# A two-layer decoder trunk: gates projected with the values, values in three column passes, background work at other turns

## The chip, the core and the metric

The kernel runs on one core of a Trainium2 chip. PE is the matmul engine, DVE the vector engine, ACT the scalar engine, POOL is GpSimd, and SP issues most DMAs. The metric is the device time of one execution in microseconds (us). Before the change three runs gave a median of 2369.42 us (2369.24 to 2374.68).

## What is computed

A trunk of two layers over 1024 tokens of 1024 features, in fp32. Layer 0 is an mLSTM, a matrix memory worked on in chunks of 128 tokens, followed by a squared-ReLU MLP. Layer 1 is causal attention over a shared low-rank K/V, followed by an MLP. Scales and shifts of the norms come from a conditioning vector. The part that the change touches most:

```
q, k, v, ig, fg, og = split(h @ w_in)        # 512, 512, 1024, 8, 8, 1024 columns
i_pre = ig + gate_b[0];  f_pre = fg + gate_b[1]
# per chunk of 128 tokens and per head (8 heads, dk 64, dv 128):
log_d   = b[t] - b[s] + i[s], -inf where s > t   # b: running sum of log sigmoid(f)
w_intra = exp(log_d - m[t])
s       = (q k^T) * w_intra
num     = w_inter * (q C) + s v
C_new   = decay * C + sum_s w[s] k[s] v[s]^T     # the state carried to the next chunk
h       = num / max(|den|, exp(-m))
out     = (rmsnorm(h) * sigmoid(og)) @ w_out
```

In layer 1 a block of 128 queries scores against the keys up to its own last token, so the last piece of keys is 128, 256, 384 or 512 wide.

## The kernel before

Tokens are worked on in two halves of 512 (`hfs[0]`, `hfs[1]`, called half 0 and half 1). Every large product is in three matmuls on a high and a low part of each operand (`mm3`, L230 to L234: L232, L233, L234). A weight tile is loaded by `wload` into a `raw` buffer (four of them), ACT casts its high part (L189), DVE subtracts to get the low part (L190), and the pair goes to a `ws` buffer (eight, so four pairs). In most projections the weight is the stationary operand and 512 tokens stream; in V the tokens are stationary and 256 weight columns stream.

PSUM has three pools of two tiles: `ps` and `pc` (one bank each) and `pm` (two banks each). Instructions are recorded step by step by generators, and a scheduler then places them into one queue for each engine, which runs in order. `weave` and `in_turn` take turns between two generators; `with_bg(g, bgs, n)` takes n steps of the background generator for each step of g. The background holds the scales and shifts of the norms (`ada_chunk`, DVE multiply-adds L358 and L360 over weight rows, then four transposes L340).

The stages of layer 0, by time in the trace of before:

- q and k of half 0 (to 80 us), then its gates: `gates_in` (L626) puts 16 gate columns in a weight tile of 128 mostly zero columns and runs 16 matmuls of L642 and L643 for a half, each 512 wide; `gates0` (L702) then computes on 8 partitions.
- V of half 0 (`v_in`, L657) from 84 to 147 us, taken in turns with `intra0` (L761). For each head `intra0` puts a row of gate sums (L775) and the causal mask (L772, bf16) into one PSUM bank, ACT takes exps (L779); for each pair of heads it makes 64-row scores (L787), which DVE multiplies by the exps (L792).
- `og0` (L690), the output gate, taken in turns with `chunks0` (L814), to 217 us. In `chunks0` the 64-row products with the state are L831, the 128-row products L836.
- gates, q and k, then V of half 1, with `split_o` (L801) of half 0 between.
- the first MLP, half 0, from about 540 to 846 us. `two_streams` (L2028) steps the dense generator `f0` and another one in turns. There the other is `behind` (L2078), which draws steps from `bg_latent`: the rest of the background, then `latent_weights` (L1322), which has six turns. A turn loads a weight tile, sums its rows on DVE (L1336, L1338 seven times), scales it (L1341), splits it (L190), then turns the sums with a transpose (L1346) and reduces them (L1347). In the trace they run between 736 and 804 us. `with tc.issue_after` in `go` (L2011) keeps PE's order as recorded.

In layer 1, `score_mm` (L1506) makes five matmuls for each piece of keys (L1517 to L1520, L1523), and a piece is at least 256 wide.

Of the kernel before, what the change touches and what calls it, by code (L numbers as in the profile page):

```python
# [9 lines left out]
F32 = mybir.dt.float32  # L10
# [72 lines left out]
def kernel(  # L83
# [542 lines left out]
    def gates_in(hf):  # L626
        h = hf.h
        wg = raw(F32R).rearrange("p (a b) -> p a b", b=P)
        nc.gpsimd.memset(wg.bitcast(F32), 0.0)
        rg = tmp()  # L630
        rgv = rg[:, :128].rearrange("p (k n) -> p k n", n=16)
        nc.sync.dma_start(rgv, wcols(w_in, 2048, 16))
        for g in range(2):
            s = ts(g, 8)
            nc.scalar.copy(wg[:, :, 32 * g : 32 * g + 8], rgv[:, :, s])
            nc.vector.tensor_sub(
                wg[:, :, 64 + 32 * g : 72 + 32 * g], rgv[:, :, s],
                wg[:, :, 32 * g : 32 * g + 8].bitcast(F32),
            )
        gp = ps()  # L640
        for k in range(KD):
            nc.tensor.matmul(gp, wg[:, k], h.lo[k], start=k == 0, stop=False)  # L642
# [14 lines left out]
    def v_in(hf):  # L657
        h = hf.h
        hf.v = []
        last = sb.tile([P, 4, VE], F32, tag="v8", bufs=1, name=f"v8_{next(uid)}")  # L660
        nc.gpsimd.memset(last[:, :, 128:VE], 1.0)
        for t in range(4):
            v = k4()[:, : 7 * VE].rearrange("p (h e) -> p h e", e=VE)
            nc.gpsimd.memset(v[:, :, 128:VE], 1.0)
            hf.v.append([v[:, h_] for h_ in range(7)] + [last[:, t]])
            hf.v[t].append(v)
        for j in range(4):
            w0 = wload([(0, 0, wcols(w_in, 1024 + j * 256, 256, 0, 4))], 256)
            w1 = wload([(0, 0, wcols(w_in, 1024 + j * 256, 256, 4, 4))], 256)
            for t in range(4):  # L670
                pt = ps()[:, :256]
                for k in range(KD):
                    w = w0 if k < 4 else w1
                    mm3(
                        pt, h.hi[k][:, ts(t, P)], h.lo[k][:, ts(t, P)],
                        w[0][:, k % 4], w[1][:, k % 4], k == 0, k == KD - 1,
                    )
                i = pt.rearrange("p (a b) -> p a b", b=P)
                if j < 3:
                    parts = [(hf.v[t][8][:, 2 * j : 2 * j + 2, 0:128], i)]  # L680
                else:
                    parts = [(hf.v[t][6 + e][:, 0:128], i[:, e]) for e in range(2)]
                for o, a in parts:
                    if t % 2:
                        nc.vector.tensor_copy(o, a)
                    else:
                        nc.scalar.copy(o, a)
                yield

    def og0(hf, alloc):  # L690
        hf.gs = FH(F32, alloc)
        for k in range(NH):
            pt = proj_fm(w_in, 2064 + k * P, hf.h)
            g = hf.gs[k]
            nc.scalar.activation(g, pt, AF.Exp, scale=-1.0)  # L695
# [6 lines left out]
    def gates0(hf):  # L702
# [3 lines left out]
        t1, t2, t3 = r8(), r8(), r8()  # L706
        nc.vector.tensor_copy(t1, gp[64:72])
        nc.vector.scalar_tensor_tensor(t1, gp[0:8], col(GB, 1)[0:8], t1, ALU.add, ALU.add)
        nc.vector.tensor_copy(t2, gp[96:104])
        nc.vector.tensor_copy(t3, gp[32:40])  # L710
        nc.vector.scalar_tensor_tensor(t2, t3, col(GB + 1, 1)[0:8], t2, ALU.add, ALU.add)
        ig, fg = t1, t2
# [48 lines left out]
    def intra0(hf):  # L761
# [3 lines left out]
        for p_ in range(4):  # L765
# [3 lines left out]
            for r in range(2):  # L769
                hh = 2 * p_ + r  # L770
                pt = pc()
                nc.tensor.matmul(  # L772
                    pt, maskA, identb.unsqueeze(1).to_broadcast([P, 4, P]), start=True, stop=False
                )
                nc.tensor.matmul(  # L775
                    pt, e8[:, hh : hh + 1].to_broadcast([P, P]), RM, start=False, stop=True
                )
# [5 lines left out]
                yield  # L783
            st = pm()
            for j in range(4):
                for r in range(2):
                    nc.tensor.matmul(  # L787
                        st[:, r, ts(j, P)], kp[ts(r, 64), ts(j, P)], qp[ts(r, 64), ts(j, P)],
                        start=True, stop=True,
                    )  # L790
            for r in range(2):
                nc.vector.tensor_mul(PT[:, r], st[:, r], E[r])  # L792
                yield
            pt = pc()
            nc.tensor.matmul(pt, selW[:, p_], RM, start=True, stop=True)
# [18 lines left out]
    def chunks0(hf):  # L814
# [4 lines left out]
        for j in range(4):  # L819
            g = hf.i * 4 + j  # L820
            cs = ts(j, P)
            v = hf.v[j]
            nvs = []
            for q in range(2):
                num = pm()
                nv = num[:, :, 0 : 2 * VE].rearrange("p b (i e) -> p b i e", e=VE)
                for i in range(2):
                    p_ = 2 * q + i

                    for r in range(2 if g > 0 else 0):  # L830
                        nc.tensor.matmul(  # L831
                            nv[:, r, i], hf.q[p_ // 2][ts(r, 64), p_ % 2, cs],
                            Cst[ts(r, 64), p_], start=True, stop=False,
                        )
                    for r in range(2):
                        nc.tensor.matmul(  # L836
                            nv[:, r, i], hf.PT[p_][:, r, cs], v[2 * p_ + r],
                            start=g == 0, stop=True,
                        )
                nvs.append(nv)  # L840
            if g < 7:
# [664 lines left out]
    def score_mm(o2, kk, q, kn, i):  # L1506
# [424 lines left out]
    drain(with_bg(gates_in(hfs[0]), bgs, 1))  # L1931
    x1 = load_x1()
    drain(weave(with_bg(v_in(hfs[0]), bgs, 1), intra0(hfs[0]), 1.5))
    y1 = rms_x1(x1)
# [36 lines left out]
    so = split_o(hfs[1])  # L1971
    for k, _ in enumerate(og0(hfs[1], k4v)):
        if k % 2:
# [53 lines left out]

    def two_streams(dense, other, fill=iter(()), more=4):  # L2028

# [4 lines left out]
        while True:  # L2034
# [5 lines left out]
            while n == "align" and at[0] != "hid" or n != "align" and n > 0:  # L2040
# [60 lines left out]
    drain(p1)  # L2101
    two_streams(with_weight_sums(f0), behind(bg_latent(), 4))
    rope_perm()
# [132 lines left out]
```

## Time and profile before

| | |
|---|---|
| median of three runs | 2369.42 us |
| the profiled execution | 2373.3 us |
| its span | 2371.2 us |
| mean granted PE clock | 0.996 |
| DMA, mean | 177 GB/s |

The page lists the busy time of each engine over the span, the chain of work that ended last, and the costliest groups of instructions. A row of a group reads: line, engine, operation, output <- inputs, shape, count | busy us, mean ns of one | idle time before them and what ended it. PE matmuls overlap, so the mean of one is longer than the step from one start to the next. A row of the timeline reads: start, length, engine, line, operation, and in brackets the idle time before it. A row of the waits reads: total us, times, longest.

### The profile page before, as it was taken

Reading aid. Unit: us, or ns where it says so; the run is one execution under the profiler, and the core shown is the slowest. Engines: PE = TensorE matmul, PEld = TensorE weight load, DVE = VectorE, ACT = ScalarE, POOL = GpSimd, SP = SyncE. Lnnn points to the kernel's source line nnn. Section 1 sums busy time; section 2 is a strip of 40 time slices with the busy share of each in tenths; the row PEclk is TensorE's granted clock in tenths of the full one; section 3 lists DMA queues with packets and bytes.
Section 4 is the critical chain, followed back from the end, with each engine's and each line's share of the span. In section 5 each row is a group of like instructions: output and inputs, shape, how many; then the busy total and the mean of one; then the engine's idle time right before and its main releaser. Section 6 shows DMA issues by size and latency. Waiting matters only on the chain.

```text
span 2371.2 us, 32533 instructions
## 1 busy us (share of the span) xinstructions
PE 2334.8 (98%) x12197; PEld 1967.3 (83%) x12197; DVE 1605.2 (68%) x2657; ACT 1099.8 (46%) x1826; POOL 147.6 (6%) x345
## 2 busy tenths in 40 slices
PE   7999999999999999999999999999999999999998
PEld 5888888788888888888888888888888888989997
DVE  6667866868666677877774967766566478457556
ACT  4355334655333464434444544434434445655543
POOL 1000000000001210111110110001001000000000
PEclk9999999999999999999999999999999999999999
DMA  9453564544656966667754675885544552657552
GB/s 312 143 145 89 181 184 137 170 130 150 187 178 166 313 184 197 185 200 205 227 157 117 196 208 176 269 272 167 173 129 132 147 169 86 189 175 218 165 183 89
DMA packets 408350, 420.77 MB, mean 177 GB/s; under 512 B 27427, under 2 KB 310112, under 8 KB 404608
## 3 DMA queue, kind: packets, MB, share of 16 engines
q1 hardware_dynamic: 402272, 385.02, 51.9%
q0 software_dynamic: 5920, 33.66, 6.5%
q8 instruction: 96, 1.57, 0.3%
q14 instruction: 62, 0.51, 0.1%
HBM read 359.37 MB, written 92.80 MB: 191 GB/s over the span
## 4 chain that ended last, share of the span: by engine, by line
PE 90%; DVE 4%; DMA 3%; ACT 2%; issue 1%; SPq 0%; DVEq 0%; ACTq 0%
PE ps L232 16%; PE ps L233 15%; PE ps L234 15%; PE pm L232 10%; PE pm L233 10%; PE pm L234 10%; PE pc L234 2%; PE pc L232 2%; PE pc L233 2%; DMA raw<-in_mlp_w_dram 1%; PE pc L1637 1%; DMA raw<-in_a_w_in_dram 1%; DVE wl L190 1%; PE pm L836 1%; PE pm L1523 1%
## 5 line engine op out<-in xcount | busy, mean ns | idle before, releaser
L190 DVE TENSOR_TENSOR wl<-raw,wh 128x1024 fp32r<-128x1024 f32 (+2 forms) x382 | 458.5, 1203 | 385.8 <-ACT wh L189 281.4
L189 ACT CAST wh<-raw 128x1024 fp32r<-128x1024 f32 (+2 forms) x382 | 394.0, 1035 | 657.9 <-PE ps L232 241.8
L232 PE MATMUL ps<-k,wl 128*128 128x512 f32 (+1 forms) x1464 | 560.3, 383 | 2.6 <-ACT k L695 1.4
L234 PE MATMUL ps<-k,wh 128*128 128x512 f32 (+1 forms) x1464 | 551.6, 377 | 0.0
L233 PE MATMUL ps<-k,wh 128*128 128x512 f32 (+1 forms) x1464 | 550.7, 376 | 0.0
L232 PEld LDWEIGHTS ps<-k,wl 128*128 128x128 f32 x1464 | 275.7, 188 | 56.5 <-issue 3.6
L234 PEld LDWEIGHTS ps<-k,wh 128*128 128x128 f32 x1464 | 275.5, 188 | 51.7 <-issue 0.7
L233 PEld LDWEIGHTS ps<-k,wh 128*128 128x128 f32 x1464 | 275.9, 188 | 50.0 <-issue 1.9
L198 DVE TENSOR_TENSOR k<-k,pm 128x512 f32<-128x512 f32 (+1 forms) x254 | 211.2, 860 | 87.2 <-PE pm L234 86.1
L232 PE MATMUL pm<-hd,wl 128*128 128x512 f32 x512 | 201.1, 393 | 0.5 <-ACT hd L472 0.5
L233 PE MATMUL pm<-hd,wh 128*128 128x512 f32 x512 | 199.5, 390 | 0.2 <-DVE hd L473 0.2
L234 PE MATMUL pm<-hd,wh 128*128 128x512 f32 x512 | 199.4, 390 | 0.0
L232 PE MATMUL pm<-wh,hd 128*128 128x512 f32 x488 | 192.2, 394 | 3.9 <-ACT raw L1529 3.7
L233 PE MATMUL pm<-wl,hd 128*128 128x512 f32 x488 | 190.5, 390 | 0.0
L234 PE MATMUL pm<-wh,hd 128*128 128x512 f32 x488 | 190.3, 390 | 0.0
L360 DVE SCALAR_TENSOR_TENSOR tma<-raw,cond,tma 128x512 f32<-128x512 f32 x168 | 125.7, 748 | 20.0 <-DMA raw<-in_kv_ada_w_dram 13.8
L1529 ACT ACTIVATE raw<-pm,sm 128x128 f32<-128x128 f32 (+3 forms) x64 | 47.4, 741 | 155.1 <-DVE sm L1528 118.2
L473 DVE TENSOR_TENSOR hd<-tmp,hd 128x512 fp32r<-128x512 f32 x128 | 88.0, 689 | 40.4 <-ACT hd L472 39.8
L232 PEld LDWEIGHTS pm<-hd,wl 128*128 128x128 f32 x512 | 96.2, 188 | 20.9 <-ACT hd L472 0.9
L233 PEld LDWEIGHTS pm<-hd,wh 128*128 128x128 f32 x512 | 96.2, 188 | 20.5 <-DVE hd L473 0.5
L234 PEld LDWEIGHTS pm<-hd,wh 128*128 128x128 f32 x512 | 96.2, 188 | 20.2
L985 POOL COPY sm<-sm 128x1 f32<-128x1 f32 x128 | 51.9, 412 | 967.2 <-DVE sm L984 930.3
(385 smaller groups left out, 4064.1 us busy)
## 6 DMA issues: line engine op xcount, KB each, us to landing
raw<-in_mlp_w_dram SPq DMA_DIRECT2D x240, 512.0 KB, 4.3
raw<-in_ada_w_dram SPq DMA_DIRECT2D x80, 512.0 KB, 4.3
raw<-in_a_w_in_dram SPq DMA_DIRECT2D x48, 512.0 KB, 4.8
sums<-in_mlp_w_dram POOLq DMA_DIRECT2D x96, 256.0 KB, 4.8
raw<-sums SPq DMA_DIRECT2D x64, 256.0 KB, 3.7
xs<-k SPq DMA_DIRECT2D x40, 256.0 KB, 3.6
raw<-in_kv_ada_w_dram SPq DMA_DIRECT2D x16, 512.0 KB, 3.9
raw<-in_a_w_out_dram SPq DMA_DIRECT2D x16, 512.0 KB, 5.0
```

The source lines that it names most:

```text
L189: nc.scalar.copy(hi[:, :n], r[:, :n])
L190: i = nc.vector.tensor_sub(lo[:, :n], r[:, :n], hi[:, :n].bitcast(F32))
L198: return f(*a, **k)
L232: nc.tensor.matmul(o, ll, rh, start=start, stop=False, **m)
L233: nc.tensor.matmul(o, lh, rl, start=False, stop=False, **m)
L234: pe_last[0] = nc.tensor.matmul(o, lh, rh, start=False, stop=stop, **m)
L360: nc.vector.scalar_tensor_tensor(acc, r[:, kk], cond[:, k : k + 1], acc, ALU.mult, ALU.add)
L473: nc.vector.tensor_sub(lo, u, hi.bitcast(F32))
L836: nc.tensor.matmul(nv[:, r, i], hf.PT[p_][:, r, cs], v[2 * p_ + r], start=g == 0, stop=True,)
L985: now = nc.gpsimd.tensor_copy(seen, flag)
L1523: nc.tensor.matmul(o[:, :w], qh, kh, start=False, stop=True)
L1529: nc.scalar.activation(pr[:, :n], f, AF.Exp, bias=m, scale=SCALE, accum_out=l)
```

## The change

The gates' 16 columns are taken along as columns 256 to 271 of V's first pass, with tokens stationary, and turned by four transposes for each half. V is made in three passes, of 2, 3 and 3 heads, into two `pm` tiles. The mask matmul goes; POOL sets the values after the diagonal to zero, behind the product with the scores. The scores of a pair go to two `ps` banks. `chunks0` issues its 64-row products by fours, then its 128-row products by fours. Every second `og0` tile of half 1 goes to a `pm` bank. `score_mm` takes 128 columns where there are no more. The background has other rates, in half 1 it runs from q and k on, `behind` aligns once at its start, and takes two steps of the background a turn where it took four.

```diff
     def gates_in(hf):
...
-        gp = ps()
-        for k in range(KD):
-            nc.tensor.matmul(gp, wg[:, k], h.lo[k], start=k == 0, stop=False)
-            nc.tensor.matmul(gp, wg[:, k], h.hi[k], start=False, stop=k == KD - 1)
+        gp = pc()
+        for t in range(4):
+            nc.tensor.transpose(gp[0:64, ts(t, P)], hf.graw[:, t], ident)
         hf.gp = gp
...
+        for h0, nh, kg in ((6, 2, 3), (0, 3, 2), (3, 3, 2)):
+            n = nh * P + (16 if h0 == 6 else 0)
+            b = [pm(), pm()]
+            for k0 in range(0, KD, kg):
+                nk = min(kg, KD - k0)
+                w = wload([(0, 0, wcols(w_in, 1024 + h0 * P, n, k0, nk))], n)
+                for t in range(4):
+                    for k in range(nk):
+                        kk = k0 + k
+                        mm3(
+                            b[t // 2][:, t % 2, :n], h.hi[kk][:, ts(t, P)], h.lo[kk][:, ts(t, P)],
+                            w[0][:, k], w[1][:, k], kk == 0, kk == KD - 1,
+                        )
...
-    def og0(hf, alloc):
+    def og0(hf, alloc, wide=False):
...
-            pt = proj_fm(w_in, 2064 + k * P, hf.h)
+            pt = proj_fm(w_in, 2064 + k * P, hf.h, (lambda: pm()[:, 0]) if wide and k % 2 else ps)
...
                 nc.tensor.matmul(
-                    pt, maskA, identb.unsqueeze(1).to_broadcast([P, 4, P]), start=True, stop=False
-                )
-                nc.tensor.matmul(
-                    pt, e8[:, hh : hh + 1].to_broadcast([P, P]), RM, start=False, stop=True
+                    pt, e8[:, hh : hh + 1].to_broadcast([P, P]), RM, start=True, stop=True
                 )
...
-            st = pm()
+            st = [ps(), ps()]
...
+            causal = PT.rearrange("p r (j t) -> p (r j) t", t=P)
+            nc.gpsimd.affine_select(
+                out=causal, in_=causal, pattern=[[0, 8], [1, P]], compare_op=ALU.is_ge,
+                fill=0.0, base=0, channel_multiplier=-1,
+            )
...
-            w = max(256, min(512, n - g * 512))
+            w = min(512, n - g * 512)
...
-    drain(gates_in(hfs[1]))
-    main = chain(twice(qk_in(hfs[1])), v_in(hfs[1]))
-    for _ in range(4):
+    v1 = v_in(hfs[1])
+    for _ in range(6):
+        next(v1)
+    main = chain(with_bg(twice(qk_in(hfs[1])), bgs, 1.6), with_bg(v1, bgs, 1.1))
+    scored = chain(gates_in(hfs[1]), intra0(hfs[1]))
+    next(scored)
+    for n in range(8):
         next(main)
-    drain(split_o(hfs[0]))
-    for _ in range(2):
-        next(main)
-    drain(weave_n(with_bg(main, bgs, 1.7), intra0(hfs[1]), 0.8))
+        if n == 1:
+            drain(split_o(hfs[0]))
+    drain(weave_n(main, scored, 0.95), scored)
...
-    def two_streams(dense, other, fill=iter(()), more=4):
+    def two_streams(dense, other, fill=iter(()), more=2):
...
-                if at[0] == "hid":
+                if at[0] != "within":
                     some(fill, per)
...
     def behind(fill, per):
 
+        yield "align"
         more = True
         while more:
-            yield "align"
             more = some(fill, per)
             yield 1
...
-    two_streams(with_weight_sums(f0), behind(bg_latent(), 4))
+    two_streams(with_weight_sums(f0), behind(bg_latent(), 2))
```

Three places in the engines' queues. In the rows the names are out<-in with buffer numbers, and after the change the lines from L690 to L1350 have other numbers: L1344 is the transpose L1346 of before, L1345 the reduction L1347, L1334 and L1336 the sums L1336 and L1338, L1339 the scaling L1341, and L808 is L811.

PE at the end of the first MLP's half 0, before: the last of six turns of `latent_weights`, between two dense tiles.

```order
L232 MATMUL pm_7086<-hd_6844,wl_6983 128x512
L233 MATMUL pm_7086<-hd_6844,wh_6982 128x512
L234 MATMUL pm_7086<-hd_6844,wh_6982 128x512
L1346 MATMUL pc_7117<-ident,tma_7022 128x128
L232 MATMUL ps_7127<-k_730_4356,wl_7041 128x512
L233 MATMUL ps_7127<-k_731_4357,wh_7040 128x512
```

The transposes of the six turns stand 48 dense matmuls apart there, and 192 dense matmuls of half 0 follow the last. PE at the end of half 0 now; `ps_7274` is half 1's first tile:

```order
L234 MATMUL pm_7097<-hd_6860,wh_7009 128x512
L1344 MATMUL pc_7128<-ident,tma_7050 128x128
L1344 MATMUL pc_7149<-ident,tma_7133 128x128
L1344 MATMUL pc_7170<-ident,tma_7154 128x128
L1344 MATMUL pc_7191<-ident,tma_7175 128x128
L232 MATMUL ps_7274<-k_841_4747,wl_7258 128x512
L233 MATMUL ps_7274<-k_842_4748,wh_7257 128x512
```

Four of the six transposes now stand behind the last dense matmul of half 0, with no matmul between them.

DVE at the same place, now: from the add behind the last dense matmul on, the first two of the four turns.

```order
L198 TENSOR_TENSOR k_772_4386<-k_772_4386,pm_7097 128x1024
L1345 TENSOR_REDUCE lbias<-pc_7128 128x1
L1334 TENSOR_SCALAR tma_7133<-raw_7131,ada 128x128
L1336 SCALAR_TENSOR_TENSOR tma_7133<-raw_7131,ada,tma_7133 128x128
L459 TENSOR_TENSOR tmc_7232<-tmc_7232,tmc_7249 128x512
L1336 SCALAR_TENSOR_TENSOR tma_7133<-raw_7131,ada,tma_7133 128x128
L459 TENSOR_TENSOR tmc_7232<-tmc_7232,tmc_7252 128x512
L1336 SCALAR_TENSOR_TENSOR tma_7133<-raw_7131,ada,tma_7133 128x128 x5
L1339 TENSOR_TENSOR raw_7131<-raw_7131,mods 128x1024
L1345 TENSOR_REDUCE lbias<-pc_7149 128x1
L1334 TENSOR_SCALAR tma_7154<-raw_7152,ada 128x128
```

And DVE's rows at the end of the last turn, before half 1's first tile gets its low part `wl_7258`:

```order
L1336 SCALAR_TENSOR_TENSOR tma_7175<-raw_7173,ada,tma_7175 128x128 x2
L190 TENSOR_TENSOR wl_7165<-raw_7152,wh_7164 128x1024
L1336 SCALAR_TENSOR_TENSOR tma_7175<-raw_7173,ada,tma_7175 128x128 x5
L1339 TENSOR_TENSOR raw_7173<-raw_7173,mods 128x1024
L1345 TENSOR_REDUCE lbias<-pc_7191 128x1
L190 TENSOR_TENSOR wl_7186<-raw_7173,wh_7185 128x1024
L190 TENSOR_TENSOR wl_7258<-raw_7255,wh_7257 128x1024
```

What stood among the adds of a running MLP before stands in one piece between the last dense matmul of half 0 and the low part that half 1's first matmul reads.

DVE at the gates of half 1, before: from the first step on the gates' PSUM tile (`ps_2169`) on.

```order
L707 COPY tmc_2186<-ps_2169 8x512
L708 SCALAR_TENSOR_TENSOR tmc_2186<-ps_2169,cols,tmc_2186 8x512
L709 COPY tmc_2187<-ps_2169 8x512
L710 COPY tmc_2188<-ps_2169 8x512
L711 SCALAR_TENSOR_TENSOR tmc_2187<-tmc_2188,cols,tmc_2187 8x512
L190 TENSOR_TENSOR wl_2424<-raw_2421,wh_2423 128x1024
```

The same place now; `pc_2181` holds the turned gates, and the next low part `wl_2386` stands after the rows shown, behind six more of the kinds L360, L722, L725 and L729.

```order
L704 TENSOR_SCALAR tmc_2186<-pc_2181,cols 8x512
L705 COPY tmc_2188<-pc_2181 8x512
L706 TENSOR_SCALAR tmc_2187<-tmc_2188,cols 8x512
L710 SCALAR_TENSOR_TENSOR tmc_2188<-tmc_2187 8x512
L808 TENSOR_TENSOR k_403_2271<-hd_988,k_402_2270 128x1024
L712 TENSOR_SCALAR tmc_2192<-tmc_2188 8x512
L808 TENSOR_TENSOR k_405_2273<-hd_1074,k_404_2272 128x1024
L714 SCALAR_TENSOR_TENSOR tmc_2188<-tmc_2192,tmc_2188 8x512
L808 TENSOR_TENSOR k_407_2275<-hd_1136,k_406_2274 128x1024
L715 SCALAR_TENSOR_TENSOR tmc_2193<-tmc_2187,tmc_2193 8x512
L342 TENSOR_REDUCE sm_2331<-pc_2326 128x4
```

The low part of the next weight has moved from behind five short steps to behind the gate steps, the four low parts of `split_o` and a turn of the background.

More of the change, by code (lines that the diff above doesn't have):

```diff
@@ L822, in chunks0 @@
             v = hf.v[j]
[L823 to L827, printed above, removed]
+            nums = [pm(), pm()]
+            nvs = [
+                num[:, :, 0 : 2 * VE].rearrange("p b (i e) -> p b i e", e=VE) for num in nums
+            ]
+            for i in range(2):
+                for q, nv in enumerate(nvs if g > 0 else []):
                     p_ = 2 * q + i
-                    for r in range(2 if g > 0 else 0):
+                    for r in range(2):
                         nc.tensor.matmul(
@@ L834, in chunks0 @@
                         )
+                for q, nv in enumerate(nvs):
+                    p_ = 2 * q + i
                     for r in range(2):
@@ L839, in chunks0 @@
                         )
-                nvs.append(nv)
             if g < 7:
@@ L1930 @@
         )
-    drain(with_bg(gates_in(hfs[0]), bgs, 1))
+    main = with_bg(v_in(hfs[0]), bgs, 0.73)
+    for _ in range(6):
+        next(main)
     x1 = load_x1()
-    drain(weave(with_bg(v_in(hfs[0]), bgs, 1), intra0(hfs[0]), 1.5))
+    scored = chain(gates_in(hfs[0]), intra0(hfs[0]))
+    next(scored)
+    for _ in range(5):
+        next(main)
+    drain(weave(main, scored, 1.9))
     y1 = rms_x1(x1)
@@ L1938 @@
     drain(n1)
-    drain(gates_in(hfs[1]))
-    main = chain(twice(qk_in(hfs[1])), v_in(hfs[1]))
-    for _ in range(4):
+    v1 = v_in(hfs[1])
+    for _ in range(6):
+        next(v1)
+    main = chain(with_bg(twice(qk_in(hfs[1])), bgs, 1.6), with_bg(v1, bgs, 1.1))
+    scored = chain(gates_in(hfs[1]), intra0(hfs[1]))
+    next(scored)
+    for n in range(8):
         next(main)
-    drain(split_o(hfs[0]))
-    for _ in range(2):
-        next(main)
-    drain(weave_n(with_bg(main, bgs, 1.7), intra0(hfs[1]), 0.8))
+        if n == 1:
+            drain(split_o(hfs[0]))
+    drain(weave_n(main, scored, 0.95), scored)
     drain(bg0)
@@ L1971 @@
     so = split_o(hfs[1])
-    for k, _ in enumerate(og0(hfs[1], k4v)):
+    for k, _ in enumerate(og0(hfs[1], k4v, True)):
         if k % 2:
```

63 lines of the change are left out of this document (23 added, 40 removed).

## The prediction

> **What bounds the kernel now.** I read the page's busy times first, then its chain that ended last, then one window of a dense stage.
>
> ```profile
> PE 2334.8 (98%) x12197; PEld 1967.3 (83%) x12197; DVE 1605.2 (68%) x2657; ACT 1099.8 (46%) x1826; POOL 147.6 (6%) x345
> ```
>
> ```profile
> PE 90%; DVE 4%; DMA 3%; ACT 2%; issue 1%; SPq 0%; DVEq 0%; ACTq 0%
> ```
>
> ```profile
> 1900.00:2000.00 100.00, 100.00 (x439) 82.12 (x438) 85.52 (x122) 53.67 (x79) 0.00 (x0) 1.00 0.43 134
> ```
>
> PE sets the end: 98% busy, 90% of the chain. In the window (length, sum, then PE, PEld, DVE, ACT, POOL, clock, DMA share, GB/s) it does 439 512-column matmuls in 100 us at full clock: **0.228 us each**. So an edit counts in two ways: matmuls that go or come, at their step from start to start, and holes in PE's queue. DVE at 86% in that window tells that a hole can come from DVE: it has little slack beside dense work. The steps:
>
> ```profile
> 111.88 0.28 PE L232 MATMUL ps<-wh,k 128*128 128x256 f32 x1
> 112.00 0.28 PE L233 MATMUL ps<-wl,k 128*128 128x256 f32 x1
> 112.12 0.39 PE L772 MATMUL pc<-identb,maskA 128*128 128x512 bf16 x1
> 112.16 0.58 PE L775 MATMUL pc<-RM,e 128*128 128x512 f32 x1
> 112.58 0.28 PE L234 MATMUL ps<-wh,k 128*128 128x256 f32 x1
> ```
>
> A 256-column matmul starts 0.12 us after the last. The pair of mask (L772) and gate row (L775) takes 112.58 - 112.12 = 0.46 us; less one of 0.228, the mask costs 0.23. By the straight line through 0.228 (512) and 0.120 (256), 384 columns cost 0.174 and 272 cost 0.127.
>
> **The change, part by part: PE's work.**
>
> ```profile
> L642 PE MATMUL ps<-k,raw 128*128 128x512 f32 x16 | 6.3, 397 | 0.0
> L772 PE MATMUL pc<-identb,maskA 128*128 128x512 bf16 x16 | 6.2, 387 | 0.5 <-ACT tmc L779 0.5
> L232 PE MATMUL ps<-wh,k 128*128 128x256 f32 x288 | 82.7, 288 | 0.8 <-DVE k L685 0.8
> L1523 PE MATMUL pm<-k,k 128*128 128x256 f32 x32 | 11.8, 369 | 0.0
> ```
>
> The gates' own matmuls go: 16 of L642 and as many of L643, 32 x 0.228 = -7.3 us. The masks go: 16 x 0.23 = -3.7. Values (V): by the loops, 2 halves x 4 column blocks x 4 row blocks x 24 = 768 matmuls of 256 columns (92.2 us; the 288 of L232 hold 256 of them) become 192 of 272 and 384 of 384 (24.4 + 66.8 = 91.2): -1.0. Scores: in 32 units the last piece of keys is 256 wide (L1523); in half of them 128 would do, so 16 x 5 = 80 matmuls shrink. What 128 columns cost, and what a change of array shape costs, these rows bear on:
>
> ```profile
> 164.21 0.49 PE L831 MATMUL pm<-Cst,k 64*128 64x130 f32 x4
> 164.64 0.71 PE L836 MATMUL pm<-k,hd 128*128 128x130 f32 x4
> 165.28 0.49 PE L831 MATMUL pm<-Cst,k 64*128 64x130 f32 x4
> 165.70 0.66 PE L544 MATMUL ps<-ident,k 128*128 128x128 f32 x4
> 166.20 0.28 PE L836 MATMUL pm<-k,hd 128*128 128x130 f32 x1
> ```
>
> Four 128-column transposes (L544) fill 0.50 us behind a change from 64-row tiles, 0.125 each; I take 0.11 without it. The scores then save 80 x 0.01 = -0.8; the ends are the straight line's 0.066 (-4.3) and as dear as 512 columns (+8.6). The 8 new transposes of gate rows cost +1.0. There and back between 64-row and 128-row work takes 165.28 - 164.21 = 1.07 us. The work in it is four matmuls at 0.11 and four that run two at a time, some 0.67, so a change of shape costs about 0.20. Chunk products by fours, the two banks of scores and the new turns leave 112 runs of one shape where there were 126: 14 x 0.195 = -2.7 (ends 0 and -5.5). Work on PE: -7.3 - 3.7 - 1.0 - 0.8 + 1.0 - 2.7 = **-14.5**.
>
> **Old holes that go.**
>
> ```profile
> PE ps L232 <- ACT k L695: 1.4, 1, 1.4
> PE ps L232 <- DVE wl L190: 1.0, 1, 1.0
> PE ps L232 <- DVE k L685: 0.8, 1, 0.8
> PE pc L340 <- DVE tma L360: 1.1, 1, 1.1
> ```
>
> These are PE's waits for V's evacuations, for the weights behind the gates and for a background turn. Their places are rewritten; I let all go: **-4.3** (end: 0).
>
> **New hole 1, behind half 0's V.** Before, og0's first tile stood ready at once. Now V ends with two of the four head pairs of `intra0` still to do, and og0 wants the `ps` banks that their scores hold.
>
> ```profile
> L779 ACT ACTIVATE tmc<-pc,gc 128x128 f32<-128x128 f32 x64 | 18.0, 371 | 13.4 <-PE pc L775 13.4
> L792 DVE TENSOR_TENSOR hd<-pm,tmc 128x512 f32<-128x512 f32 x16 | 10.9, 686 | 3.6 <-ACT tmc L779 3.6
> L398 POOL TENSOR_SCALAR_AFFINE_SELECT tmp<-tmp 128x128 f32<-128x128 f32 x1 | 0.3, 305 | 0.0
> ```
>
> Sixteen exps go by in fours of about 1.12 us (0.371 each, overlapped), 4.5 us; four products on DVE 2.7; two scalings of q (the same shape) 1.4; two causal selects by POOL. A select of 128x1024 is eight times the one of 0.305 if it grows with its columns (2.4 us); a short fixed part would leave 1.1; I take 1.7, twice: 3.4. That is 12.0 us in line, against some 6.2 us of PE's own work in it (rows of scores, gate rows and scalings at the steps above). **+5.8**, ends 2.4 (the selects beside everything) and 7.2.
>
> **New hole 2, half 1's gates.** The order shows on DVE, between the end of the gate transposes and the low weight part that PE wants next, eight 8x512 steps, four low parts of `split_o` (L811), five background steps (L360), ten short ones and the low part itself. Before, the low part stood behind five.
>
> ```profile
> 225.47 0.68 DVE L707 COPY tmc<-ps 8x512 f32<-8x512 f32 x1
> 229.03 1.21 DVE L190 TENSOR_TENSOR wl<-raw,wh 128x1024 fp32r<-128x1024 f32 x1
> 230.17 0.67 DVE L715 SCALAR_TENSOR_TENSOR tmc<-tmc 8x512 f32<-8x512 f32 x1
> 231.54 0.41 DVE L717 TENSOR_SCALAR tmc<-tmc 8x512 f32<-8x512 f32 x1 [0.70 <-ACT tmc L716]
> 248.53 3.11 DVE L360 SCALAR_TENSOR_TENSOR tma<-raw,cond,tma 128x512 f32<-128x512 f32 x4
> L811 DVE TENSOR_TENSOR k<-hd,k 128x1024 fp32r<-128x1024 f32 x8 | 9.7, 1208 | 0.0
> ```
>
> 8 x 0.72 + 4 x 1.21 + 5 x 0.78 + 10 x 0.36 + 1.2 = 19.3 us. PE has 54 matmuls and four transposes to do meanwhile, 54 x 0.228 + 0.4 = 12.7: **+6.5**. Two tiles on, the queue is still behind; there I take **+4.2** (ends 0 and another 6.5).
>
> **New hole 3, the end of the first MLP, half 0.** Before, the six turns of `latent_weights` stand 48 dense matmuls (11 us) apart and the last has 192 behind it. With one `align` at the start and two steps a turn, four are left over at the end: four transposes (L1346) in a row on PE, and nothing dense between. What one such turn costs DVE is shown where it was hidden:
>
> ```profile
> 747.11 1.22 DVE L198 TENSOR_TENSOR k<-k,pm 128x1024 f32<-128x1024 f32 x1 [2.80 <-PE pm L234]
> 748.25 0.28 DVE L1347 TENSOR_REDUCE lbias<-pc 128x1 f32<-128x128 f32 x1
> 748.45 0.28 DVE L1336 TENSOR_SCALAR tma<-raw,kvada 128x128 f32<-128x128 f32 x1
> 748.76 2.68 DVE L1338 SCALAR_TENSOR_TENSOR tma<-raw,kvada,tma 128x128 f32<-128x128 f32 x7
> 751.47 1.23 DVE L1341 TENSOR_TENSOR raw<-raw,mods 128x1024 f32<-128x1024 f32 x1
> L459 DVE TENSOR_TENSOR tmc<-tmc,tmc 128x512 f32<-128x512 f32 x21 | 14.5, 690 | 1.7 <-ACT tmc L455 1.2
> ```
>
> DVE cannot begin before the last dense matmul, for which its L198 waits. From there, by starts: L198 1.14; the first turn 0.20 + 0.31 + 2.71 + 1.2 and two L459 of 0.69 between, 5.8; two turns with a low part (1.15) in each, 5.57 twice; at the end 0.20 and two low parts, 2.5. The last of these is what half 1's first tile waits for. Together 20.6 us on DVE alone; 1.5 for the hand-offs and for a weight load that is issued late: **+22.1**, ends 20.6 and 27 (a whole 4.3 us of landing, by the page's DMA rows, behind the last but one).
>
> **What such holes do to the clock.**
>
> ```profile
> 1579.89 0.55 PE L1519 MATMUL pm<-hd,k 128*128 128x512 f32 x1 [1.07 <-DMA k<-td]
> 1580.20:1583.60 3.40, 3.40 (x12) 2.86 (x11) 0.86 (x2) 0.00 (x0) 0.00 (x0) 0.50 1.04 425
> 1583.60:1587.00 3.40, 3.40 (x19) 2.83 (x18) 1.74 (x5) 1.51 (x3) 0.00 (x0) 1.00 1.01 411
> ```
>
> After a hole PE ran 3.4 us at clock 0.50: 1.7 us lost. Holes 2 (twice) and 3 cost 3 x 1.7 = **+5.1**. The Trainium skill ("TensorE: Matmul & The Clock Gate", Part 1, What's actually happening) has the half clock come after an idle window of some 3.4 us. The row quoted shows it behind a hole of only 1.07, so the trace asks for less. By the page the three holes alone count, as I count them; by the row the pieces of hole 1 would count too, 1.7 more.
>
> **The sum.** -14.5 - 4.3 + 5.8 + 6.5 + 4.2 + 22.1 + 5.1 = **+24.9 us**. The profiled execution took 2373.3 us (span 2371.2), 3.9 more than the median of the runs, 2369.4; so 2398.2 against the one and **2394.3** against the other, which I give.
>
> **The rivals.**
> - *128-column scores cost as much as 512.* For it: no row shows this type at that width. Against: transposes of that width step at 0.11. It adds 9.4: 2403.7.
> - *Half 1's gates stay hidden*, should DVE reach them earlier than PE does. For it: a low part of a weight may wait four tiles ahead in the buffers. Against: the order. It takes away 10.7 and two clock windows, 3.4: 2380.2.
> - *The causal select holds DVE up.* Each would stop, for its 1.7 us, a DVE step that reads two operands from SBUF, such as the low part that og0 waits for; two of them count: 2397.7. The Trainium skill ("SBUF — State Buffer", Who interferes with whom) has GpSimd and a DVE step with two SBUF inputs shut each other out for a whole instruction. No run here shows it.
> - *Hole 3 alone is not there*, if the four last turns find DVE free before the last dense matmul. That leaves 2394.3 - 22.1 - 1.7 = 2370.5, no change. The order speaks against it.
> - *The other side: DVE is never late*, in hole 3 and hole 2 alike. Then -14.5 - 4.3 + 5.8 = -13.0: 2356.4, faster. It decides from the point where both queues end before PE's work does, 6.5 and 22 us sooner than I have them.
>
> **How the numbers follow.** About 0.3%, 7 us, is what a measurement of this kernel can tell from no change. Forecast 0.55, dear scores 0.14, hidden gates 0.14, the select 0.04: all slower, 0.87. Hole 3 gone 0.07: the same. Never late 0.06: faster. The range 2376 to 2408 takes in the first four; its lower end is hidden gates with hole 1 at its low end, its upper end dear scores with a late load in hole 3.
>
> **What would show it.** Right: in the changed profile one hole of PE of about 22 us behind four transposes in a row, released by DVE's low weight part, with DVE busy all through it; holes of 4 to 7 us at half 1's first projection tiles; clock 0.5 behind each; no L642; 80 score matmuls of 128 columns at a step of 0.11. Wrong: PE busy through the end of half 0's MLP, or a step near 0.23 at 128 columns. If PE's busy work falls by far more than 14.5 us, the cost of a change of array shape is what I have too low.

## The result, and the profile after

The changed kernel takes 2408.72 us (median of 5 runs, 2406.79 to 2413.36), the kernel before 2370.44 (5 runs). The ratio is **1.0157**, 95% interval 1.0141 to 1.0173: slower by 38 us. Its profiled execution took 2406.79 us, with a span of 2405.1. That execution lies 1.9 us under its median and that of before 2.9 over its own, so the two traces differ by only 33.9 us in span. The readings below explain those 33.9.

The page's first part and its chain, as for before:

```profile
PE 2331.5 (97%) x11965; PEld 1965.9 (82%) x11965; DVE 1602.3 (67%) x2655; ACT 1098.1 (46%) x1824; POOL 152.8 (6%) x353
PE 87%; DVE 5%; DMA 4%; ACT 2%; issue 1%; SPq 0%; POOL 0%; DVEq 0%; ACTq 0%; POOLq 0%
```

PE has 232 matmuls less and is still 34 us longer on its way: the time went into holes, and into the half clock behind them. What PE waited for (total us, times, longest), the first rows of the list:

```profile
PE pc L1344 <- DVE tma L1336: 15.9, 3, 5.9
PE ps L232 <- DVE wl L190: 14.7, 4, 5.3
...
PE pm L835 <- POOL hd L787: 3.6, 2, 3.3
...
PE pc L892 <- DVE tmc L866: 2.8, 1, 2.8
```

The longest entry of this list before was 3.8 us. To see where the time stands, the span is cut at instructions that both programs have: ACT's first exps of og0 for half 0's first and last tile and half 1's first tile, and DVE's first product L473 of the first MLP's half 0 and half 1. The table holds the length of each stretch before, and for every later kernel its difference from that, all from the profiled executions (us). A row is one execution: most of them lie within 3.0 us of their kernel's median, f2's lies 5.5 above its own.

```
                          to og0  og0,chunks  to half 1's  og0,wout  MLP 0,   rest    span
                          half 0  half 0      og0          half 1    half 0
before                     153.8     64.9       187.0        92.9     355.3  1517.1
after                       +3.5     -1.3        +7.1        -1.7     +28.1    -1.8   +33.9
e1_old_pace                 +2.8     -1.4        +8.7        -1.7      +5.0    +0.2   +13.6
e2_new_pace_in_before       +0.1     +0.0        +0.1        +0.0     +12.2    -3.9    +8.6
f2_split_early              +3.9     -1.4       +13.2        -1.7      +7.4    +3.1   +24.5
f1_split_and_bg_late        +2.0     -1.3       +20.8        -0.2      +7.1    -3.0   +25.3
g1_old_h1_order             +3.4     -1.4        +9.5        -1.7      +7.7    +0.6   +18.1
g2_h0_scores_sooner         +1.0     -1.4       +12.5        -1.7      +6.9    +2.3   +19.6
p3_select_in_before         -3.5     +0.0        -2.5        +0.0      +2.6    +2.5    -0.8
e3_narrow_and_fours         +0.2     -1.7        -3.5        +0.0      +0.5    -1.9    -6.4
k1_three_passes_alone       -2.7     +0.7       +12.6        -0.6      +2.4    +0.9   +13.3
k6_five_raw_buffers         +5.4     +0.3        +4.8        -1.2      -1.2    -0.3    +7.7
k2_parts_that_pay           -2.5     -1.7        -2.9        -1.7      +4.9    -2.2    -6.1
k3_background_in_chunks     -2.8     -1.7        +5.7        -1.7      -1.7    -1.7    -4.0
```

Nearly all of the loss is in the first MLP's half 0 (+28.1) and in half 1's projections (+7.1). The timeline of PE at the end of that half 0:

```profile
851.70 0.40 PE L234 MATMUL pm<-hd,wh 128*128 128x512 f32 x1
851.94 0.27 PE L1344 MATMUL pc<-ident,tma 128*128 128x128 f32 x1
858.13 0.47 PE L1344 MATMUL pc<-ident,tma 128*128 128x128 f32 x1 [5.92 <-DVE tma L1336]
863.59 0.48 PE L1344 MATMUL pc<-ident,tma 128*128 128x128 f32 x1 [4.99 <-DVE tma L1336]
869.04 0.47 PE L1344 MATMUL pc<-ident,tma 128*128 128x128 f32 x1 [4.97 <-DVE tma L1336]
874.44 0.79 PE L232 MATMUL ps<-k,wl 128*128 128x512 f32 x1 [4.92 <-DVE wl L190]
```

and two windows of it, with the next 3.5 us:

```profile
852.00:874.50 22.50, 1.70 (x6) 0.60 (x4) 20.19 (x39) 5.33 (x6) 0.00 (x0) 0.60 0.76 244
874.50:878.00 3.50, 3.50 (x8) 2.75 (x9) 0.00 (x0) 0.00 (x0) 0.00 (x0) 0.50 0.97 232
```

From the first transpose to half 1's first matmul 22.5 us pass, in which DVE is busy for 20.2 and PE for 1.7; then PE runs at clock 0.50.

### The profile page after: what moved, and what is told of

Its sections match the earlier page's. It is cut to its first block, busy times and chain, and to the rows that moved or that the text cites. A ratio compares the mean times of both kernels' runs of the same rounds, so it can differ in the third digit from the quotient of the medians.

```text
span 2405.1 us, 32159 instructions
## 1 busy us (share of the span) xinstructions
PE 2331.5 (97%) x11965; PEld 1965.9 (82%) x11965; DVE 1602.3 (67%) x2655; ACT 1098.1 (46%) x1824; POOL 152.8 (6%) x353
## 4 chain that ended last, share of the span: by engine, by line
PE 87%; DVE 5%; DMA 4%; ACT 2%; issue 1%; SPq 0%; POOL 0%; DVEq 0%; ACTq 0%; POOLq 0%
PE ps L232 14%; PE ps L233 13%; PE ps L234 13%; PE pm L232 11%; PE pm L233 11%; PE pm L234 11%; DMA raw<-in_mlp_w_dram 2%; PE pc L234 2%; PE pc L232 2%; PE pc L233 2%; PE pc L1635 1%; ACT wh L189 1%; DVE wl L190 1%; DVE sm L1525 1%; PE pm L835 1%
## 5 line engine op out<-in xcount | busy, mean ns | idle before, releaser
L232 PE MATMUL ps<-k,wl 128*128 128x512 f32 (+1 forms) x1432 | 550.2, 384 | 14.8 <-DVE wl L190 14.7
L234 PE MATMUL ps<-k,wh 128*128 128x512 f32 (+1 forms) x1432 | 541.9, 378 | 0.0
L233 PE MATMUL ps<-k,wh 128*128 128x512 f32 (+1 forms) x1432 | 541.3, 378 | 0.0
L234 PEld LDWEIGHTS ps<-k,wh 128*128 128x128 f32 x1432 | 271.3, 189 | 50.8 <-issue 0.7
L233 PEld LDWEIGHTS ps<-k,wh 128*128 128x128 f32 x1432 | 272.1, 190 | 49.3 <-issue 1.7
L360 DVE SCALAR_TENSOR_TENSOR tma<-raw,cond,tma 128x512 f32<-128x512 f32 x168 | 126.2, 751 | 20.9 <-DMA raw<-in_ada_w_dram 10.5
L232 PEld LDWEIGHTS pm<-hd,wl 128*128 128x128 f32 x512 | 96.2, 188 | 20.8 <-ACT hd L472 0.9
L473 DVE TENSOR_TENSOR hd<-tmp,hd 128x512 fp32r<-128x512 f32 x128 | 88.1, 690 | 37.0 <-ACT hd L472 36.5
```

The costliest lines, as they stand in the source:

```text
L232: nc.tensor.matmul(o, ll, rh, start=start, stop=False, **m)
L233: nc.tensor.matmul(o, lh, rl, start=False, stop=False, **m)
L234: pe_last[0] = nc.tensor.matmul(o, lh, rh, start=False, stop=stop, **m)
L360: nc.vector.scalar_tensor_tensor(acc, r[:, kk], cond[:, k : k + 1], acc, ALU.mult, ALU.add)
L473: nc.vector.tensor_sub(lo, u, hi.bitcast(F32))
```

## The experiments

Each kernel was timed against before on the same chip; the ratio to before stands with its 95% interval in brackets.

**e1: the old pace of `behind` in the changed kernel.**

```diff
-        yield "align"
         more = True
         while more:
+            yield "align"
             more = some(fill, per)
...
-behind(bg_latent(), 2))
+behind(bg_latent(), 4))
```

> After, with the old `behind` (an align in every turn, four background steps a turn). Theory: the hole at the end of the first MLP's half 0 comes only from four `latent_weights` turns left behind the last dense matmul; in the order all six stand 48 dense matmuls apart again, so the hole of 22.5 us and the 4 us of half clock and late weights behind it go: 2408.7 - 26.6 = 2382 (2378 to 2386). Rival: DVE is simply too full in this stage, the turns among the dense matmuls make it late there, and only half comes back: about 2395.

2387.5 us, 1.0066 [1.0051, 1.0081]. Between the two, nearer the theory but outside its range: in the MLP's half 0 23.1 us come back, and the list of waits at its end holds none behind `latent_weights` any more. But 5.0 of the 28.1 stay, and 2.8 are lost elsewhere.

**e2: the new pace alone, in before.** The same lines as in e1, the other way.

> Before, with the new `behind` alone (one align, two background steps a turn). Theory: the pace is not enough by itself, what counts is how much background is left when the MLP begins; in this order one turn, not four, stands behind the last dense matmul of half 0. Then a hole of some 3.5 us and some half clock: 2370.4 + 4 = 2374 (2371 to 2378). Rival: the new pace itself costs the 26 us wherever it is used: 2390 or more.

2381.55 us, 1.0042 [1.0027, 1.0057]. Between the two: +12.2 in the MLP's half 0. The pace costs by itself, about half of the 23.1 that e1 gives back in the changed kernel, and in another way. There is no hole at the end; PE waits among the dense work, from 800 to 850 us, for low weight parts and for one transpose:

```profile
PE pm L232 <- DVE wl L190: 7.3, 3, 2.8
PE pc L1346 <- DVE tma L1338: 1.2, 1, 1.2
```

What the background's turns (L340, 4 transposes each) and the six turns of `latent_weights` do in that stretch, one kernel a pair of rows: before, e2, e1, after. A row gives the count, the length in ns, and the first and last start.

```profile
L340 PE MATMUL pc<-ident,tma x24: 270/272/328, 579.5 to 692.4; 128*128 128x128 f32 x24
L1346 PE MATMUL pc<-ident,tma x6: 270/271/271, 746.9 to 802.3; 128*128 128x128 f32 x6
```

```profile
L340 PE MATMUL pc<-ident,tma x24: 270/272/273, 579.7 to 726.6; 128*128 128x128 f32 x24
L1346 PE MATMUL pc<-ident,tma x6: 270/270/327, 800.2 to 857.2; 128*128 128x128 f32 x6
```

```profile
L340 PE MATMUL pc<-ident,tma x28: 270/272/328, 577.1 to 715.7; 128*128 128x128 f32 x28
L1344 PE MATMUL pc<-ident,tma x6: 270/270/271, 770.3 to 825.6; 128*128 128x128 f32 x6
```

```profile
L340 PE MATMUL pc<-ident,tma x28: 269/272/273, 578.9 to 756.2; 128*128 128x128 f32 x28
L1344 PE MATMUL pc<-ident,tma x6: 271/374/477, 829.8 to 869.0; 128*128 128x128 f32 x6
```

Before, six turns are left, 22.6 us apart (112.9 / 5). The new pace puts them 29.4 apart (146.9 / 5), and the new rates leave seven, not six. Alone, either (the pace in e2, the rest of the change in e1) still lets the turns end with work beside them, the last of e2 just behind half 0's last dense matmul (+12.2 and +5.0); together they push four turns of `latent_weights` past the last dense matmul. So +28.1 is more than the sum of the two, 17.2.

**f2 and f1: half 1's gates.** Both on top of e1. f2 drains `split_o` ahead of the gates; f1 puts it at the sixth step and keeps the background out of the first eight steps.

```diff
+    drain(split_o(hfs[0]))                # f2
     next(scored)
...
-    main = chain(with_bg(twice(qk_in(hfs[1])), bgs, 1.6), with_bg(v1, bgs, 1.1))
+    qk1 = twice(qk_in(hfs[1]))            # f1: eight steps of qk1 alone, then
+    main = chain(with_bg(qk1, bgs, 2.4), with_bg(v1, bgs, 1.5))
```

> e1_old_pace, with `split_o` of half 0 drained ahead of half 1's gates. In the order the four low parts L808 (4.8 us) are gone from between the gate steps and the low weight part; the background steps stay. If split_o is what made the first hole (5.4 us) at half 1's gates, it shrinks to about 0.6 and half a clock window goes: e1 less 5 to 7, 2376. If the background makes it, nothing changes: 2382.

2391.9 us, 1.0087 [1.0066, 1.0107].

> e1_old_pace, with `split_o` at the sixth step and no background in the first eight q/k steps of half 1 (rates 2.4 and 1.5 behind them). In the order the low weight part stands behind three gate steps. Theory (DVE's queue makes both holes at half 1's gates, 5.4 and 3.4 us, and the half clock behind them): e1 less 8 to 12, about 2371. Rival: the background that is packed tighter makes new holes in q/k and V of half 1, and nothing is won: 2380 or more.

2399.04 us, 1.0121 [1.0101, 1.0141]. Both misses, on the rivals' side: nothing is won. f1 is slower than e1, and its stretch to half 1's og0 loses 20.8 us where e1's loses 8.7. For f2 a loss against e1 isn't shown: the two intervals overlap, and its +13.2 comes from the execution that lies 5.5 us above the median. In f1 the first hole at the gates is gone, and one of 6.9 us stands at 275 us instead; in f2 the two holes are 3.9 and 3.8 us where e1 has 5.0 and 2.5. Reordering what DVE does there only moves the hole.

**g1 and g2: the old order of half 1, and half 0's scores begun sooner.** g1 is e1 with half 1's steps as they stood before; g2 is g1 with two steps of V, not five, ahead of half 0's `intra0`.

```diff
+    main = chain(twice(qk_in(hfs[1])), v1)      # g1
+    drain(gates_in(hfs[1]))
+    for _ in range(4):
+        next(main)
+    drain(split_o(hfs[0]))
+    for _ in range(2):
+        next(main)
+    drain(weave_n(with_bg(main, bgs, 1.7), intra0(hfs[1]), 0.8))
...
-    for _ in range(5):                          # g2
+    for _ in range(2):
         next(main)
-    drain(weave(main, scored, 1.9))
+    drain(weave(main, scored, 1.7))
```

> e1_old_pace, with half 1 again in the old order: gates drained, then q/k without background for four steps, `split_o`, two more, then V and `intra0` with 1.7 background steps a step. Theory: the stretch from half 0's last og0 to half 1's first og0 lost 7 us in the changed kernel because background, `split_o` and gate steps stand together on DVE; with the old order it comes back to the time of before or less (16 gate matmuls and 8 masks gone there, -5.5), and as the same background as before is left for the MLP, the MLP's half 0 loses 5 less: 2387.5 - 12 to 17 = 2370 to 2376. Rival: the gates that now come behind V's first pass are what costs, whatever the background does: 2384 or more.

2390.65 us, 1.0085 [1.007, 1.01]. A miss, at the rival's time: with the old order the stretch still loses 9.5 us.

> g1_old_h1_order, with half 0's `intra0` begun after two further V steps instead of five (1.7 steps a step). Theory: the holes behind half 0's V (3.3 + 1.2 + 0.8 us in the changed kernel) come from two head pairs left over; begun sooner, no pair is left and 4 to 5 us come back: g1 less 4, about 2368. Rival: ACT and DVE cannot make the pairs faster than that beside V's weights, and the holes move into V: no change against g1.

2392.18 us, 1.0093 [1.0078, 1.0108]. The stretch to half 0's og0 does get 2.4 us shorter (+1.0 for +3.4), about half of what was expected, and half 1's stretch, not touched, 3.0 longer: the whole gains nothing.

**p3 and e3: the small parts, in before.** p3 takes out the mask matmul and adds POOL's select, with the scores in their old tile; e3 has 128-column scores and `chunks0` by fours. Edits as in the change.

> Before, with the causal mask matmul taken out and POOL's select in its place, scores still in the two-bank tile. Theory: 16 matmuls of 0.23 go, and the select (1.09 us in the changed kernel) stands beside V: 2370.6 - 3.7 = 2367. Rival: the select stands in line before the product with V and holds chunks0 up as in the changed kernel (3.3 us behind POOL, in both halves): 2373.

2370.68 us, 0.9999 [0.999, 1.0009]. Between the two: the whole wins nothing. 6.0 us come in before half 1's og0, more than the masks' 3.7, and 2.6 go in the MLP, 2.5 behind it. Nine changes of array shape fewer stand in PE's queue ahead of that og0 (116 where there were 125); at the prediction's 0.195 each they would be another 1.8.

> Before, with 128-column scores and chunk products by fours. Theory: 14 changes of array shape at 0.195 us and 80 matmuls 0.01 us shorter: -3.5, 2367. In the changed kernel the stretch of half 0's og0 and chunks took 1.3 us less, which speaks for about 1 us a half. Rival: the first two-bank tile is ready no sooner and the state update waits longer: 2371 or more.

2366.49 us, 0.9983 [0.9971, 0.9995]. The whole is as the theory had it; 5.2 us of it are in the two stretches with chunks, about twice the theory's 2.7. The theory took its 14 changes of shape from the whole change. In this kernel's trace PE has 8 fewer in the first of the two stretches (26 for 34) and 18 fewer in the second (42 for 60), so 1.7 and 3.5 us come to 0.21 and 0.19 each: the price was right, the count was not.

**k1: V's three passes alone, in before**, without the gate columns. V has 22 steps a half now where it had 16, so the rates of the background and of `intra0` beside it are lowered.

```diff
-        for j in range(4):
-            w0 = wload([(0, 0, wcols(w_in, 1024 + j * 256, 256, 0, 4))], 256)
-            w1 = wload([(0, 0, wcols(w_in, 1024 + j * 256, 256, 4, 4))], 256)
...
+        for h0, nh, kg in ((6, 2, 3), (0, 3, 2), (3, 3, 2)):
+            n = nh * P
+            b = [pm(), pm()]
...
-            st = pm()
+            st = [ps(), ps()]
...
-    drain(weave(with_bg(v_in(hfs[0]), bgs, 1), intra0(hfs[0]), 1.5))
+    drain(weave(with_bg(v_in(hfs[0]), bgs, 0.73), intra0(hfs[0]), 1.1))
...
-    drain(weave_n(with_bg(main, bgs, 1.7), intra0(hfs[1]), 0.8))
+    drain(weave_n(chain(with_bg(qk1, bgs, 1.7), with_bg(v_in(hfs[1]), bgs, 1.24)), intra0(hfs[1]), 0.65))
```

> Before, with V in three passes into `pm` tiles (without the gate columns, which keep their own matmuls), scores in `ps` banks, and the rates set so that as many background and `intra0` steps fall on V as before. Theory now: half 1's stretch is slower by the passes themselves, since a weight tile lasts PE 24 x 0.174 = 4.2 us instead of 5.8, and ACT's cast, DVE's low part, the background and intra0 no longer fit beside it: +4 to +8 in the stretch from half 0's last og0 to half 1's first, 2377. Rival: it is the gates that come behind V's first pass; then the passes alone cost nothing, 2370 (PE's work -1.0).

2388.99 us, 1.0079 [1.0065, 1.0094]. The theory's side, at more than its size: with these rates the passes alone lose 12.6 us in half 1's stretch, while the gates have their old place. So the gates' place isn't needed for the loss there. PE's waits from 215 to 420 us in k1:

```profile
PE ps L232 <- DVE wl L190: 4.7, 2, 2.8
PE pm L232 <- ACT wh L189: 4.3, 2, 3.1
```

Weights are late. What ACT waited for from 215 to 405 us, before and then in k1:

```profile
ACT wh L189 <- DMA raw<-in_a_w_in_dram: 16.2, 9, 6.4
```

```profile
ACT wh L189 <- DMA raw<-in_a_w_in_dram: 44.0, 11, 8.5
```

ACT's cast waits for the load. Weights and background share four `raw` buffers; whether the load waits for one of these is what k6 tries.

**k6: k1 with five `raw` buffers**, paid for with one `tmc` and one `tmp`.

```diff
-RAW = 4
-TMP = 3
-TMC = 6
+RAW = 5
+TMP = 2
+TMC = 5
```

> k1_three_passes_alone with five raw buffers instead of four (paid for with one tmc and one tmp buffer). In k1, ACT's cast waits 44 us for weight loads in half 1's stretch where before it waits 16, and SP issues those loads only when DVE's background step has freed a raw buffer. Theory: the passes need 11 loads a half for 8, out of four buffers that the background shares; with a fifth buffer the loads go out a tile earlier, and the stretch from half 0's last og0 to half 1's first (12.6 us over before in k1) loses half or more of that: 2389 - 6 to 10 = 2379 to 2383. Rival: DVE itself is late there, whatever the buffers: no change, 2389; or the two buffers taken away make intra0 and the gates slower, over 2390.

2379.13 us, 1.0033 [1.002, 1.0046]. As the theory had it: half 1's stretch loses 4.8, not 12.6. PE's waits in it now:

```profile
PE pm L232 <- DVE v L688: 2.7, 1, 2.7
PE pm L232 <- DVE k L690: 2.5, 1, 2.5
```

No wait for a weight is left in the list: these two are for V's own evacuation, and a third, of 0.2, is for a step of the gates. Half 0's stretch became 8 us longer than in k1; whether that is the missing `tmc` and `tmp` was not tried apart. ACT's own total wait for loads hardly fell (41.7 us): it shows less than PE's list.

**k2 and k3: the parts that pay.** k2 is before with the edits of p3 and e3, and og0's second bank. k3 is k2 with the background drawn beside half 1's chunks.

```diff
     in_turn(
-        wout(...), chunks0(hfs[1]), iter(())
+        wout(...), chunks0(hfs[1]), bgs
     )
```

> Before, with the parts that cost no place in a queue: 128-column scores, chunk products by fours, the causal select by POOL for the mask matmul, and every second og0 tile of half 1 in the other pool. By the stretches of the earlier runs: -3.5 and -2.5 before og1 by the select, -1.5 and -1.9 by chunks, -1.7 by og0, 2 to 3 by scores: 2371 - 9 = 2360 to 2363. Rival: the time won before the MLP comes back as holes at its background turns, as with the select alone (2.6 of 6): 2366.

2365.63 us, 0.9982 [0.9973, 0.9991]: faster than before by 4 us, at the rival's time. 8.8 us are won ahead of the MLP and 4.9 given back in it:

```profile
PE pc L340 <- DVE tma L360: 4.2, 2, 2.9
```

> k2_parts_that_pay, with a background step beside each of half 1's chunk steps (12 steps, two turns), a stage in which DVE was 67% busy. Theory: two turns fewer are left for the first MLP's half 0, whose holes before the background transposes (1.3 and 2.9 us in k2) go with them: 4 to 5 less there, 2361. Rival: the chunk stage's own DVE steps come later for them and PE waits there instead: 2366 or more.

2371.97 us, 1.0008 [0.9999, 1.0017]. Each side had half. With five background turns left for the MLP's half 0, where k2 has six, that half falls by 6.6 against k2, and the chunk stage rises by 8.6, with this wait in it:

```profile
PE pc L897 <- DVE tmc L871: 6.2, 2, 3.2
```

## Why the prediction was right, and where its sizes were off

It said slower by 24.9 us; the medians differ by 38.3 and the traces by 33.9. The direction and the chief mechanism were right; the size fell short. The time of 2408.7 us stands at the upper end of the range, 2408 (by the ratio, on the 2369.4 that the prediction went by, 2406.6). That the range reaches so far is luck in part: its upper end was built from dear scores and a late load in hole 3, and the scores were not dear.

- **Hole 3**, +22.1 with 1.7 of half clock: right in place and cause. The trace has 22.5 us and then 3.5 us at 0.50. Short by about 4: behind the hole came a further wait of 1.2 us, for a weight, and more time below full clock (0.81 from 878 to 884, which the prediction had not counted). Another 2.7 are the place of the marks: twelve more dense matmuls fall between them than before (1548 for 1536), at 0.228 each. e1 shows that the hole goes with the pace, e2 that the pace alone doesn't make it. The prediction named only the pace ("one `align` and two steps a turn"); the seventh background turn that the new rates leave for the MLP, which it left out, is the other half.
- **Hole 2**, +6.5 and +4.2 with 3.4 of half clock: right in place and cause, a little high in size. The waits were 5.26 and 3.27 us. The rows of the first, then PE's row of the second:

```profile
253.69 0.75 DVE L360 SCALAR_TENSOR_TENSOR tma<-raw,cond,tma 128x512 f32<-128x512 f32 x1
254.58 1.23 DVE L190 TENSOR_TENSOR wl<-raw,wh 128x1024 fp32r<-128x1024 f32 x1
...
255.86 0.79 PE L232 MATMUL ps<-k,wl 128*128 128x512 f32 x1 [5.26 <-DVE wl L190]
```

```profile
273.14 0.79 PE L232 MATMUL ps<-k,wl 128*128 128x512 f32 x1 [3.27 <-DVE wl L190]
```

  Behind them PE was busy all through two windows below full clock, which cost 6.0 x 0.26 + 6.5 x 0.20 = 2.9 us:

```profile
256.00:262.00 6.00, 6.00 (x20) 4.81 (x21) 5.23 (x12) 1.64 (x3) 0.00 (x0) 0.74 0.78 240
273.50:280.00 6.50, 6.50 (x24) 5.22 (x24) 1.48 (x2) 0.59 (x1) 0.00 (x0) 0.80 0.81 249
```

  What PE waited for in the whole stretch of the changed kernel, from 215 to 420 us:

```profile
PE ps L232 <- DVE wl L190: 8.5, 2, 5.3
PE pc L892 <- DVE tmc L866: 2.8, 1, 2.8
PE pm L828 <- DVE k L683: 1.3, 2, 1.1
```

  With these 12.6 us and the 2.9 the stretch's +7.1 adds up to within 0.5: the prediction's terms that fall in it (half of the gates, masks, V and transposes, and 12 changes of shape at 0.195) come to about -8, and a wait of 1.0 of before goes. The second and third row, 4.1 us, stand in the chunks of half 1, and the prediction had no term for them.

  So hole 2 is the larger part of the loss that this kernel shows there, but not the only loss that can come in its place. f2, f1 and g1 reorder the queue, the hole shrinks or moves, and the stretch is no shorter: PE then waits for ACT's casts as well (2.0, 4.5 and 4.2 us). k1 and k6 show where such a loss can come from: 11 weight loads a half where there were 8, through `raw` buffers shared with the background. The prediction had V at -1.0, as if its loads were free; alone the passes lose 12.6 in this stretch, and a fifth buffer takes 7.8 of it back. That the loads cost anything in the changed kernel itself isn't shown: no wait behind ACT's cast stands in its list.
- **Hole 1**, +5.8: the three waits there add up to 3.3 + 0.9 + 0.6 = 4.8 us, the longest behind POOL's select. The stretch lost 3.5, where the terms for it gave about nothing. What was missed is, in the main, the clock behind the hole, some 2.8 us. The prediction named 1.7 for it, by its row of a hole of 1.07, and left it out of the sum:

```profile
146.00:149.60 3.60, 2.50 (x10) 2.11 (x11) 0.67 (x3) 3.17 (x12) 0.13 (x1) 0.56 0.30 88
149.60:153.00 3.40, 3.40 (x10) 2.63 (x9) 2.75 (x14) 1.18 (x5) 0.00 (x0) 0.50 0.00 0
```

- **PE's work**, -14.5: borne out in its parts. PE's busy time falls by only 3.3 us, but the half clock above stretched it by some 8 (2.7 behind hole 3, 2.9 and 2.8 behind the others), so about 12 of the 14.5 are seen. 128-column scores step at 0.11, as taken, so the rival of dear scores is out:

```profile
1684.51 0.27 PE L1516 MATMUL pm<-k,k 128*128 128x128 f32 x1
1684.62 0.28 PE L1517 MATMUL pm<-hd,k 128*128 128x128 f32 x1
1684.73 0.27 PE L1518 MATMUL pm<-hd,k 128*128 128x128 f32 x1
```

  Products by fours save 1.3 us in half 0's stretch of the changed kernel, which has 6 changes of shape fewer (28 for 34), and 1.7 in e3. The select gives 6.0 ahead of half 1's og0 in p3, with the masks.
- **Old holes**, -4.3: og0's second bank takes 1.7 in every kernel that has it but f1 (0.2), for the wait of 1.4 behind ACT. The others went, but new ones stand at their places.
- **The rival of the select** came true as a mechanism: in the changed kernel one of half 0's four selects takes 1.96 us and three of half 1's take 1.49 to 1.75, where an undisturbed one takes 1.09 (the pairs below are of p3 and k2). Its price is within the noise of the whole. **Hidden gates**, **hole 3 gone** and **never late** did not come.

What stays open: why the MLP's half 0 gives back what is won ahead of it (2.6 in p3, 4.9 in k2). k3 shows that it hangs on the turns left there; why DVE's L360 is later when the stage begins sooner was not settled. Stretches that an edit does not touch move by up to 4 us between kernels ("rest" in the table).

## What to carry to other kernels

Background work is paced against the dense work by two numbers, the turns left and the dense steps between them; multiply them out before one is changed, since what is left at the end stands bare. Count a re-tiled projection by its weight loads as well as by its matmuls: the buffers the loads pass through can bind while PE's own sum falls. A hole can cost twice, once by its length and once by the half clock behind it. It did behind holes 1, 2 and 3 here; behind the 2.8 us at L892 in the changed kernel the clock stayed at 1.00 (359 to 366 us).

## What the runs showed of the hardware

- POOL's select of 128x1024 takes 1.09 us, not eight times the 0.305 of 128x128. In the first pair it takes 2.02, when DVE has begun a subtract of two SBUF operands just before; in the second DVE's subtract takes 2.05, not 1.22, when the select began first. The first pair is of p3, the second of k2:

```profile
116.98 1.22 DVE L190 TENSOR_TENSOR wl<-raw,wh 128x1024 fp32r<-128x1024 f32 x1
117.13 2.02 POOL L792 TENSOR_SCALAR_AFFINE_SELECT hd<-hd 128x1024 f32<-128x1024 f32 x1 [9.04 <-DVE hd L789]
```

```profile
136.90 1.09 POOL L792 TENSOR_SCALAR_AFFINE_SELECT hd<-hd 128x1024 f32<-128x1024 f32 x1 [12.26 <-DVE hd L789]
137.01 2.05 DVE L190 TENSOR_TENSOR wl<-raw,wh 128x1024 fp32r<-128x1024 f32 x1 [0.18 <-ACT wh L189]
```

  The Trainium skill ("SBUF — State Buffer", Who interferes with whom) says that whoever issues first keeps the shared ports for its whole instruction and the other blocks; both traces agree: the second to start lasts 0.93 and 0.83 us longer than it does alone, and ends 0.95 and 1.07 us after the first, about one own length (1.09 and 1.22).
- The half clock came also behind hole 1, whose longest piece was 3.31 us with 0.92 to follow, and lasted into a second window (0.56, then 0.50 up to 153 us).
